# A two-layer hybrid decoder: conditioning products over all rows, more zero products, and other piece sizes in the first chunks

## The chip, the cores and the metric

The kernel runs on one core of one Trainium2 chip. The metric is the time of one execution on the device, in microseconds; the median of several runs is given. Five engines of the core work side by side: TensorE (PE in the profile; its weight loads are PEld), VectorE (DVE), ScalarE (ACT), GpSimd (POOL) and SyncE (SP), which here issues nearly all loads.

## The reference

A decoder trunk of two layers over one sequence of 256 tokens, width 1024, in float32. A layer is a SwiGLU block, a token mixer (layer 0: stick-breaking attention, layer 1: a gated linear recurrence, RG-LRU), and another SwiGLU block. Each block's input is normalised, scaled and shifted, and its output gated, by vectors that come from one conditioning vector c:

```python
c_act = jax.nn.silu(c)
for layer in range(DEPTH):
    mod = (c_act @ mod_w[layer] + mod_b[layer]).reshape(B, N_SUB, 3, D_MODEL)
    h, g = sublayer_input(x, norm_g[layer, 0], mod[:, 0])
    x = x + MACARON_W * g * swiglu(h, ffn_w_gu[layer, 0], ffn_w_down[layer, 0])
    ...
```

with `h = rmsnorm(x, g) * (1 + scale) + shift`, and `swiglu(h) = (silu(h @ w_g) * (h @ w_u)) @ w_down`. D_FF is 2816, the recurrent width 1280. The trunk ends with one RMSNorm.

## The kernel before

The activations lie transposed: eight tiles `x[d]` of 128 features by 256 tokens. Every weight is read once from memory, in blocks of 128 by 2048 (1 MB, the ring `raw` of three buffers, issued on SP). A float32 product is made of three products at the faster format: ScalarE rounds a piece of the block to `wh` (L536), VectorE takes the rest `wl = raw - wh` (L539), and the activations are split alike into a high and a low part (`hx`, made at L674 or L859). `group` (L565) issues wh by high, wh by low, wl by high. A *plain* group (L835) is instead one float32 product with the unsplit block and unsplit activations `h0`; it needs no split of the weights.

All operations are put on a list with costs and dependences, and `schedule` makes a plan from it: it walks in planned time, gives every operation a due time (`prio`, taken back from TensorE's order and its costs), and so fixes the order in which each engine's instructions are issued. `lat` overrides the planned time from one operation's end to its users' start. On the chip each engine works through its own list in that order and waits for semaphores; set-up instructions ahead of the list (memsets and casts on GpSimd and VectorE, L460 to L482) are not in the plan.

The start, in the first block of layer 0: ScalarE issues the load of c (one row, L1328) into a tile of the ring `rawm`; TensorE runs `EARLY` zero products (`warm`, L1323), and spreads c over 128 rows by a product with ones (L1337), in two halves of 512 columns. ScalarE takes SiLU of these into `cact` (`cond`). Meanwhile x comes in two halves; VectorE and ScalarE square it, VectorE folds the squares, TensorE sums them over the rows (L642), ScalarE makes the inverse root `rst` from that. A conditioning tile (`mod_tile`, L597) is a 128 by 1024 block of `mod_w`, 512 KB, multiplied by `cact` and summed by VectorE: eight results of a scale or shift vector. Two of them, w = 1 (scale) and w = 0 (shift), are needed for every chunk k of x. `hpre` is x[k] scaled (L668), from which ScalarE and VectorE make h.

The first block's products over the first eight column blocks (`SQ`) are ordered by chunk k of x, so that work can begin as soon as chunk 0 is there. Chunk k has 16 groups, in two halves of 1 MB loaded as pieces: chunks in `SMALL` in four pieces of 512 columns, the others in two of 1024. For chunk 0 the first `PLAIN` pieces go plain. Between the halves the load order puts the conditioning tiles of chunk k+1 (`early`). From the second set of column blocks on, all products run over whole column blocks.

At the end of the RG-LRU block, `output` (L1265) makes the operand of the last projection: for every pair n2 of blocks a product (L1275), a rounding on ScalarE, and the low part on VectorE (L1281).

Of the kernel before, what the change touches and what calls it, by code (L numbers as in the profile page):

```python
# [11 lines left out]
ALU = mybir.AluOpType  # L12
# [3 lines left out]
T = 256  # L16
TX = T + 2
D = 1024
# [5 lines left out]
NB = NR // 2  # L24
# [6 lines left out]
HALF = 1024  # L31
SQ = 8
NFIRST = 2
LAT0, RATE0, RATE = 950.0, 390.0, 360.0
SMALL = (0, 7)
EARLY, MID, LATE = 4, 3, 9
AHEAD = {(1, 0): 3}
KICK0, PLAIN = (1,), 2
HXPAD, HKPAD, ARPAD = 112, 16, 56
SKIP = 1  # L40

# [322 lines left out]
def c_dve(n):  # L364
    return 68.0 + 1.042 * n
# [11 lines left out]
def trunk(ctx, tc, xT, cb, par, modw, gu0, gu, wdn, qk, wv, wo, win, wri, wout, out):  # L377
    nc = tc.nc
    act, dve, pe, pool, sp = nc.scalar, nc.vector, nc.tensor, nc.gpsimd, nc.sync
    ctx.enter_context(tc.manual_schedule())  # L380
    pr = Program()
# [4 lines left out]
    def f32(ap):  # L386
        return ap.bitcast(F32)


    def ring(name, n, cols, dt=F32, pl=const, pitch=0):  # L390
        if pitch:
            whole = pl.tile([P, n * pitch], dt, tag=name, name=name)
            tiles = [whole[:, i * pitch : i * pitch + cols] for i in range(n)]
        else:
            tiles = [pl.tile([P, cols], dt, tag=f"{name}{i}", name=f"{name}{i}") for i in range(n)]
        return Space(name, n, lambda at, _: tiles[at]), tiles

    banks, _ = ring("bank", 8, 512, pl=psum)
    banks.exclusive = True
    rawr, _ = ring("raw", 3, CH)  # L400
    modr, _ = ring("rawm", 4, D)
    whr, _ = ring("wh", 7, HALF, F32R)
    wlr, _ = ring("wl", 7, HALF, F32R)
    const.tile([P, HXPAD], F32, tag="pad0", name="pad0")
    hxr, _ = ring("hx", 20, TX, F32R, pitch=320)
    const.tile([P, HKPAD], F32, tag="pad2", name="pad2")
    hkr, _ = ring("hk", 2, T, F32R)
    sqr, _ = ring("sq", 2, T)
    ssqr, _ = ring("ssq", 2, T)
    rmsr, _ = ring("rms", 1, T)  # L410
    rstr, _ = ring("rst", 1, T)
    hpr, _ = ring("hpre", 3, T)
    bcr, _ = ring("bc", 4, 2)
    tr, _ = ring("tr", 2, T)
    sgr, _ = ring("sg", 3, T)
# [6 lines left out]
    def new_phase(r_cells, f_cells, dts=(F32R, F32)):  # L422
        k = len(phases)
        prev = phases[-1]["spaces"] if phases else ()
        ph = {"size": (r_cells, f_cells), "dts": dts}

        def view(which):
            def v(at, n):
                enter(k)
                return phase["tiles"][which][:, at * CELL : (at + n) * CELL]  # L430
            return v

        ph["spaces"] = tuple(
            Space(f"ph{k}{n}", c, view(i), prev) for i, (n, c) in enumerate((("r", r_cells), ("f", f_cells))))
        phases.append(ph)
        return ph["spaces"]
# [15 lines left out]
    def fixed(name, cols, dt=F32):  # L452
        return const.tile([P, cols], dt, tag=name, name=name)
# [9 lines left out]
    ones = fixed("ones", P)  # L463
# [40 lines left out]
    def act_dma(dst, src, r, w, lat=2600.0):  # L504
        return pr.op("ACT", 60.0, lambda: act.dma_start(dst(), src), r, w, lat=lat)
# [6 lines left out]
    def V(fn, n, r, w, cost=None, ptr=0):  # L512
        return pr.op("DVE", cost or c_dve(n) + 62.0 * ptr, fn, r, w)
# [283 lines left out]
    def ffn(l, s, nxt, hook):  # L797
# [3 lines left out]
        else:  # L801
            R, _ = new_phase(2 * NF * 2 + AHEAD.get((l, s), 0) * 9, 0)
# [7 lines left out]
        if j == 0:  # L810
# [52 lines left out]
            for k in range(KD):  # L863
                if k == 0:
                    h0 = norm_chunk((0, 0), k, q, PLAIN > 0)
                    warm(LATE, [pr.last_pe])
                    for ks in xq_parts:
                        normed(ks)
                else:
                    first_chunk(k)  # L870
                size = HALF // 2 if k in SMALL else HALF
                done = [0]

                def chain(dst, src, n, w):
                    chained(dst, src, n, w, RATE0)
                    done[0] += n

                    if done[0] % HALF == 0:
                        for w in ((2 - done[0] // HALF,) if k < 3 else (1, 0) if done[0] == HALF else ()):
                            early(k + 1, w)  # L880

                plain = PLAIN if k == 0 else 0
                ws = load(gu0[k], CH, f"gu0_{k}", chain, size, plain)
                for f in range(SQ):
                    for g in range(2):
                        i, c0 = divmod((f * 2 + g) * P, size)
                        if i < plain:
                            plain_group(accs[f], g, *ws[i], (f * 2 + g) * P)
                            continue
                        group(accs[f], (g, 0), lambda b, g=g: b[:, g * T : (g + 1) * T], ws[i],  # L890
                              lambda u, c0=c0: u[:, c0 : c0 + P], hcur[0, 0][k], lambda v: v[:, :T], T, k == KD - 1)
                        if k in KICK0 and f == g == 0:
                            kick_op(accs[f], 0, (0, 0))
            chained(lambda: pars()[:, NP0:], par, NPAR - NP0, [(pars, 1)])
            R, _ = new_phase(2 * NF * 2, 0)
# [244 lines left out]
    def rglru(l, s, nxt):  # L1140
# [124 lines left out]
        def output(n2):  # L1265
            g, t = gt[n2], th[n2]
            tt = [(t, 0), (t, 1)]
            if n2 >= NB - KEEP:
                b, g = g, rr[n2]
                rg = [(g, 0), (g, 1)]  # L1270
                A(g, b, AF.Gelu_apprx_tanh, 2 * T, [(b, (0, 0)), (b, (1, 0))], rg, table="gelu", psum=True, after=sqs)
            else:
                rg = [g]
                A(g, g, AF.Gelu_apprx_tanh, 2 * T, [g], [g], table="gelu", after=sqs)
            V(lambda: dve.tensor_tensor(t(), t(), g(), ALU.mult), 2 * T, tt + rg, tt)  # L1275
            if n2 < N32:
                y = t
            else:
                y = Buf(R, 4), Buf(R, 4)
                A(y[0], t, AF.Copy, 2 * T, tt, [y[0]])  # L1280
                V(lambda: dve.tensor_tensor(y[1](), t(), f32(y[0]()), ALU.subtract), 2 * T, tt + [y[0]], [y[1]])  # L1281
            for e in range(2):
                ys.append((y, slice(e * T, (e + 1) * T)))

# [29 lines left out]
    def chained(dst, src, n, w, rate=RATE):  # L1314
        last[:] = [dma(dst, src, n, w, last, LAT0, rate)]
# [10 lines left out]
    def first_loads(F):  # L1326
        c, b = Buf(modr), [Buf(banks), Buf(banks)]
        act_dma(lambda: c()[:1, :], cb, [], [c], 300.0)  # L1328

        def cond(h, after=()):  # L1330
            cs = slice(h * 512, (h + 1) * 512)
            A(lambda: cact()[:, cs], b[h], AF.Silu, 512, [b[h]], [(cact, h)], table="silu", psum=True, after=after)

        warm(EARLY)
        for h in range(2):
            cs = slice(h * 512, (h + 1) * 512)
            pr.op("PE", 1870.0, lambda h=h, cs=cs: pe.matmul(b[h]()[:, :], ones[:1, :], c()[:1, cs], start=True, stop=True),  # L1337
                  [c], [b[h]])
        cond(0)
        warm(MID, [pr.last_pe])  # L1340


        pairs = []
        for h, (scalar_, vector_, extra) in enumerate(((0, 2, 0), (2, 0, NP0))):
            d = 4 * h
            a0, n = d * T, 4 * T + extra
            chained(lambda a0=a0, n=n: xall[:, a0 : a0 + n], xT[:, a0 : a0 + n], n, x[d : d + 4] + [(pars, 0)] * h, RATE0)
            sq = Buf(F, 8)
            v0 = vector_ * T
            V(lambda sq=sq, a0=a0, v0=v0: dve.tensor_tensor(  # L1350
                sq()[:, v0 : v0 + 2 * T], xall[:, a0 + v0 : a0 + v0 + 2 * T], xall[:, a0 + v0 : a0 + v0 + 2 * T], ALU.mult),
              2 * T, x[d + vector_ : d + vector_ + 2], [(sq, "V")])
            for i in (scalar_, scalar_ + 1):
                o = A(lambda sq=sq, i=i: sq()[:, i * T : (i + 1) * T], x[d + i], AF.Square, T, [x[d + i]], [(sq, i)])
            if h == 1:
                cond(1, [o])
            p = Buf(F, 4)
            V(lambda sq=sq, p=p: dve.tensor_tensor(p(), sq()[:, : 2 * T], sq()[:, 2 * T :], ALU.add), 2 * T,
              [(sq, "V"), (sq, scalar_), (sq, scalar_ + 1)], [p])
            if h == 0:  # L1360
                pairs += [(p, slice(0, T)), (p, slice(T, 2 * T))]
            else:
                one = Buf(F, 2)
                fold = V(lambda p=p: dve.tensor_tensor(one(), p()[:, :T], p()[:, T:], ALU.add), T, [p], [one])
                pairs.append((one, slice(0, T)))
        ssq[0, 0] = tuple(pairs)
        pr.op("DVE", 80.0, lambda: dve.scalar_tensor_tensor(gbias(), col(OFF_MB + KD, KD), 1.0, col(OFF_NG, KD), ALU.add,
                                                            ALU.mult), [(pars, 0)], [gbias], [fold])
# [95 lines left out]
```

## Time and profile before

| | before |
|---|---|
| runs | 955.54 us median of 3 (954.9 to 956.22) |
| the profiled execution's own time | 955.21 us |
| its span, first to last instruction | 953.5 us |
| TensorE busy | 943.3 us (99%) |
| VectorE, ScalarE busy | 794.7, 568.5 us |
| memory read | 248.92 MB, 262 GB/s over the span |

Times in the profile are microseconds from the start of the span. A row of a timeline gives start, length, engine, line, operation, the tile it writes and the tile it reads, and in brackets how long the engine had been idle before and what ended that. Successive products of TensorE overlap, so the rate is read from starts, not from lengths. A row of groups gives busy time and the mean length of one in ns.

### The profile page before, as it was taken

What the parts mean: (1) busy time and instruction counts of PE and PEld (TensorE: products, weight loads), DVE (VectorE), ACT (ScalarE), POOL (GpSimd) and SP (SyncE); (2) the same over time, 40 slices, a digit from 0 to 9 for tenths busy, and PEclk for the clock granted to TensorE, in tenths of its full rate; (3) what the DMA queues carried; (4) which work ended last, traced back from release to release, by engine and by line L of the source; (5) the groups of instructions that cost most, each with busy time, mean ns of one, the idle gap of its engine ahead of it and who ended that gap; (6) DMA issues with size and microseconds to landing.
All of it is one profiled execution on the core that took longest, in us unless ns stands there. A gap on an engine that the chain in (4) does not pass through costs nothing.

```text
span 953.5 us, 19706 instructions
## 1 busy us (share of the span) xinstructions
PE 943.3 (99%) x8124; PEld 932.3 (98%) x8124; DVE 794.7 (83%) x1291; ACT 568.5 (60%) x925; POOL 2.4 (0%) x15
## 2 busy tenths in 40 slices
PE   9999999999999999999999999999999999999996
PEld 6999999999999999999999999999999999999996
DVE  7999888899999998888899998875998997555443
ACT  6685453479786755554466544535789676544343
POOL 1000000000000000000000000000000000000000
PEclk9999999999999999999999999999999999999999
DMA  9989889947754698889966999997253646545421
GB/s 349 406 314 364 322 327 358 363 147 265 259 200 155 223 362 331 322 303 349 363 256 255 335 359 333 353 337 280 90 179 131 222 175 234 210 179 206 170 110 45
DMA packets 47900, 251.25 MB, mean 264 GB/s; under 512 B 5313, under 2 KB 5953, under 8 KB 28098
## 3 DMA queue, kind: packets, MB, share of 16 engines
q1 hardware_dynamic: 47376, 249.46, 69.7%
q8 instruction: 63, 1.03, 0.4%
q10 hardware_dynamic: 434, 0.53, 0.2%
q14 instruction: 27, 0.22, 0.1%
HBM read 248.92 MB, written 1.05 MB: 262 GB/s over the span
## 4 chain that ended last, share of the span: by engine, by line
PE 90%; DVE 4%; DMA 3%; ACT 2%; issue 0%; SPq 0%; DVEq 0%
PE bank L565 85%; PE bank L950 2%; DMA raw<-in_gu 2%; DVE wl L539 1%; PE bank L1080 1%; PE bank L1023 1%; DMA arenar<-in_modw 1%; ACT arenaf L509 1%; DVE arenaf L1262 1%; PE bank L1058 1%; PE bank L1191 0%; ACT wh L536 0%; DVE arenar L1281 0%; DVE arenaf L1259 0%; PE bank L642 0%
## 5 line engine op out<-in xcount | busy, mean ns | idle before, releaser
L565 PE MATMUL bank<-hx,wh 128*128 128x256 f32 (+1 forms) x3284 | 565.0, 277 | 0.6 <-DVE hx L859 0.5
L536 ACT ACTIVATE wh<-raw 128x1024 fp32r<-128x1024 f32 (+1 forms) x326 | 336.0, 1050 | 285.9 <-PE bank L565 205.1
L565 PEld LDWEIGHTS bank<-hx,wh 128*128 128x128 f32 x3284 | 496.7, 188 | 1.3 <-DVE hx L859 1.0
L539 DVE TENSOR_TENSOR wl<-raw,wh 128x1024 fp32r<-128x1024 f32 (+1 forms) x326 | 387.8, 1210 | 114.9 <-ACT wh L536 112.2
L565 PE MATMUL bank<-hx,wl 128*128 128x256 f32 (+1 forms) x1650 | 456.8, 277 | 0.2 <-DVE wl L539 0.2
L565 PEld LDWEIGHTS bank<-hx,wl 128*128 128x128 f32 x1650 | 310.3, 188 | 0.4 <-DVE wl L539 0.4
L565 PE MATMUL bank<-arenar,wh 128*128 128x256 f32 x1696 | 289.3, 276 | 0.1
L565 PEld LDWEIGHTS bank<-arenar,wh 128*128 128x128 f32 x1696 | 255.5, 188 | 0.3 <-DVE arenar L1281 0.3
L565 PE MATMUL bank<-arenar,wl 128*128 128x256 f32 x848 | 234.1, 276 | 0.0
L597 DVE SCALAR_TENSOR_TENSOR rawm<-rawm,cact 128x1024 f32<-128x1024 f32 x128 | 154.5, 1218 | 8.8 <-DMA rawm<-in_modw 8.3
L565 PEld LDWEIGHTS bank<-arenar,wl 128*128 128x128 f32 x848 | 159.2, 188 | 0.0
L509 ACT ACTIVATE arenar<-a 128x256 fp32r<-128x256 f32 x88 | 35.2, 404 | 8.4 <-DVE a L790 8.2
L509 ACT ACTIVATE sg<-bank 128x256 f32<-128x256 f32 x82 | 30.0, 369 | 13.9 <-PE bank L565 13.9
L795 DVE TENSOR_TENSOR arenar<-a,arenar 128x256 fp32r<-128x256 f32 x88 | 36.3, 417 | 1.0 <-ACT arenar L509 1.0
L790 DVE TENSOR_TENSOR a<-bank,sg 128x256 f32<-128x256 f32 x82 | 33.9, 416 | 0.2
L712 DVE SCALAR_TENSOR_TENSOR x<-bank,mf,x 128x256 f32<-128x256 f32 x48 | 21.5, 477 | 9.1 <-PE bank L565 9.1
L509 ACT ACTIVATE hx<-x,mf 128x256 fp32r<-128x256 f32 x40 | 18.5, 500 | 17.2 <-DVE x L712 17.2
L950 PE MATMUL bank<-wh,hx 128*128 128x256 f32 x128 | 24.2, 284 | 0.2 <-DVE arenar L1088 0.2
L509 ACT ACTIVATE hx<-hpre,mf 128x256 fp32r<-128x256 f32 x41 | 19.5, 498 | 5.8 <-DVE hpre L668 5.8
L509 ACT ACTIVATE arenaf<-bank 128x384 f32<-128x384 f32 (+1 forms) x37 | 17.7, 505 | 6.2 <-DVE arenaf L1262 2.8
L950 PEld LDWEIGHTS bank<-wh,hx 128*128 128x128 f32 x128 | 20.0, 188 | 0.7 <-DVE arenar L1088 0.5
L1407 ACT ACT_TABLE_LOAD x15 | 19.2, 1283 | 1.6 <-PEq L1452 1.3
(123 smaller groups left out, 541.1 us busy)
## 6 DMA issues: line engine op xcount, KB each, us to landing
raw<-in_gu SPq DMA_DIRECT2D x79, 1024.0 KB, 5.2
rawm<-in_modw SPq DMA_DIRECT2D x128, 512.0 KB, 6.5
raw<-in_wdn SPq DMA_DIRECT2D x44, 1024.0 KB, 4.9
raw<-in_win SPq DMA_DIRECT2D x10, 1024.0 KB, 5.0
arenar<-in_modw SPq DMA_DIRECT2D x16, 512.0 KB, 10.2
raw<-in_qk SPq DMA_DIRECT2D x8, 1024.0 KB, 4.8
raw<-in_gu SPq DMA_DIRECT2D x14, 512.0 KB, 10.2
raw<-in_wout SPq DMA_DIRECT2D x5, 1024.0 KB, 4.7
```

Of the source, the lines that this page charges most:

```text
L509: act.activation(o(), i(), f, **{k: (v() if callable(v) else v) for k, v in kw.items()})
L536: act.activation(h()[:, :m], raw()[:, a : a + m], AF.Copy)
L539: dve.tensor_tensor(lo()[:, :m], raw()[:, a : a + m], f32(h()[:, :m]), ALU.subtract)
L565: pe.matmul(o(b()), wc(u()), xc(v()), start=start and n == 0, stop=stop and n == len(passes) - 1, skip_group_check=True)
L597: dve.scalar_tensor_tensor(raw(), raw(), 1.0, cact(), ALU.mult, ALU.mult, accum_out=m()[:, t : t + 1])
L712: dve.scalar_tensor_tensor(x[d](), acc.b()[:, j * T : (j + 1) * T], gate()[:, d : d + 1], x[d](), ALU.mult, ALU.add)
L790: V(lambda: dve.tensor_tensor(a(), b()[:, T:], sg(), ALU.mult), T, [(b, (1, 0)), sg], [a])
L795: V(lambda: dve.tensor_tensor(y[1](), a(), f32(y[0]()), ALU.subtract), n, [a, y[0]], [y[1]])
L950: pe.matmul(o, u()[:, tb * P : (tb + 1) * P], v()[:, c0 : c0 + 256], start=start and n == 0, stop=k == KD - 1 and n == 2, skip_group_check ...
L1023: pe.matmul(zb[e]()[:, BL[i]], v()[rows, kc], w()[rows, qc], start=False, stop=i == 1 and n == 2, skip_group_check=True)
L1058: pe.matmul(b()[:, :S], ntri, hd(q(), e), start=False, stop=False, skip_group_check=True)
L1407: act.preload_act_table_set(TABLES[t])
```

## The change

1. `EARLY` goes from 4 to 8: eight zero products before the conditioning products.
2. The first tile of the ring `rawm` is set to zero by VectorE at the start; c still fills its first row. The product with ones then runs over all 128 rows of it instead of one.
3. `PLAIN` goes from 2 to 3: three of the four pieces of chunk 0 go plain.
4. `SMALL` takes in chunk 1: it is loaded and split in four pieces of 512 columns instead of two of 1024.
5. In the load order, chunks 3 and 4 get, like the earlier ones, one conditioning tile after each half instead of both after the first.
6. The last low part of the RG-LRU output (L1281, last n2) is planned with 900 ns instead of 170 ns to its users.

```diff
-SMALL = (0, 7)
-EARLY, MID, LATE = 4, 3, 9
+LASTY = 900.0
+SMALL = (0, 1, 7)
+EARLY, MID, LATE = 8, 3, 9
-KICK0, PLAIN = (1,), 2
+KICK0, PLAIN = (1,), 3
...
-    modr, _ = ring("rawm", 4, D)
+    modr, mods = ring("rawm", 4, D)
+    dve.memset(mods[0], 0.0)
...
-                        for w in ((2 - done[0] // HALF,) if k < 3 else (1, 0) if done[0] == HALF else ()):
+                        for w in ((2 - done[0] // HALF,) if k < 5 else (1, 0) if done[0] == HALF else ()):
...
-                V(lambda: dve.tensor_tensor(y[1](), t(), f32(y[0]()), ALU.subtract), 2 * T, tt + [y[0]], [y[1]])
+                pr.op("DVE", c_dve(2 * T), lambda: dve.tensor_tensor(y[1](), t(), f32(y[0]()), ALU.subtract), tt + [y[0]], [y[1]],
+                      lat=LASTY if n2 == NB - 1 else None)
...
-            pr.op("PE", 1870.0, lambda h=h, cs=cs: pe.matmul(b[h]()[:, :], ones[:1, :], c()[:1, cs], start=True, stop=True),
+            pr.op("PE", 1870.0, lambda h=h, cs=cs: pe.matmul(b[h]()[:, :], ones, c()[:, cs], start=True, stop=True),
                   [c], [b[h]])
```

## The prediction

> **What bounds the kernel now.** I read the page's busy times and chain first, then the list of waits of TensorE, the chain in order of time, and the timelines of the first 35 us.
>
> ```profile
> span 953.5 us, 19706 instructions
> ...
> PE 943.3 (99%) x8124; PEld 932.3 (98%) x8124; DVE 794.7 (83%) x1291; ACT 568.5 (60%) x925; POOL 2.4 (0%) x15
> ...
> PE 90%; DVE 4%; DMA 3%; ACT 2%; issue 0%; SPq 0%; DVEq 0%
> ```
>
> TensorE is the bound, and the time is its work plus what it loses before and between. Every edit but one acts in the first 45 us, so the question is where TensorE loses time there. The waits of TensorE, largest in the early part, and the chain in order of time:
>
> ```profile
> PE bank L835 <- ACT hpre L509: 0.6, 1, 0.6
> PE bank L565 <- DVE hx L859: 0.5, 1, 0.5
> PE bank L565 <- DVE wl L539: 0.2, 1, 0.2
> ```
>
> ```profile
> 16.29 11.25 DMA raw<-in_gu
> ...
> 30.31 2.28 DVE arenar L597 x3
> ...
> 32.69 1.15 DVE wl L539
> ...
> 33.88 166.54 PE bank L565 x1462
> ```
>
> From 33.88 us the chain is TensorE alone, 0.1139 us a product (166.54 / 1462), 0.342 us for the three products of a split group. So whatever the change does early is worth exactly what it moves TensorE's place at 33.88 us. TensorE's timeline up to there:
>
> ```profile
> 1.16 1.04 PE L1323 MATMUL bank<-zero 128*128 128x256 bf16 x4 [1.16 <-POOL eps L462]
> 2.30 3.75 PE L1337 MATMUL bank<-rawm,ones 1*128 1x512 f32 x4
> ...
> 6.60 2.85 PE L642 MATMUL bank<-arenaf,ones 128*128 128x256 f32 x6
> 9.24 2.13 PE L1323 MATMUL bank<-zero 128*128 128x256 bf16 x9
> 11.92 3.72 PE L835 MATMUL bank<-hpre,raw 128*128 128x256 f32 x16 [0.56 <-ACT hpre L509]
> ...
> 15.29 0.59 PE L565 MATMUL bank<-hx,wh 128*128 128x256 f32 x2
> ...
> 18.30 0.28 PE L565 MATMUL bank<-hx,wh 128*128 128x256 f32 x1
> 19.11 0.39 PE L565 MATMUL bank<-hx,wh 128*128 128x256 f32 x1 [0.53 <-DVE hx L859]
> ...
> 33.26 0.40 PE L565 MATMUL bank<-hx,wh 128*128 128x256 f32 x2
> ```
>
> Three places matter: the first plain product at 11.92 us; a hole before chunk 1 (from 18.30 to 19.11 us between two starts, where 0.114 is usual: 0.70 us lost); and a hole in chunk 3 (the second product of the pair at 33.26 starts near 33.38, the next at 33.88: 0.39 us lost).
>
> **What sets 11.92 us.** ScalarE and VectorE:
>
> ```profile
> 0.79 0.52 ACTq L505 DMA_DIRECT2D rawm<-in_cb  x1
> ...
> 1.34 1.28 ACT L1407 ACT_TABLE_LOAD   x1 [1.34 <-PEq L1452]
> ...
> 4.38 0.60 ACT L509 ACTIVATE cact<-bank 128x512 f32<-128x512 f32 x1 [1.76 <-PE bank L1337]
> ...
> 4.88 0.71 ACT L509 ACTIVATE arenaf<-x 128x256 f32<-128x256 f32 x2
> ...
> 5.62 0.69 DVE L1358 TENSOR_TENSOR arenaf<-arenaf 128x512 f32<-128x512 f32 x1 [0.49 <-ACT arenaf L509]
> ...
> 9.31 1.22 DVE L597 SCALAR_TENSOR_TENSOR arenar<-arenar,cact 128x1024 f32<-128x1024 f32 x1
> ...
> 10.78 0.48 DVE L668 SCALAR_TENSOR_TENSOR hpre<-x,mf,rst 128x256 f32<-128x256 f32 x1 [0.25 <-ACT mf L509]
> ...
> 11.36 0.51 ACT L509 ACTIVATE hpre<-hpre,mf 128x256 f32<-128x256 f32 x1 [0.43 <-DVE hpre L668]
> ```
>
> The conditioning products let ScalarE's first SiLU start at 4.38. The squares of x are queued behind it on ScalarE and end at 5.59 (4.88 + 0.71). VectorE waits for them (0.49 us), and from 5.62 works without a pause until 10.53 (9.31 + 1.22); hpre follows after 0.25, the plain product 1.14 later (11.92 - 10.78). So a conditioning vector that comes late moves the whole start one for one.
>
> **The clock.** The zero products at 9.24 lie (2.13 - 0.42) / 8 = 0.214 us apart, 0.42 being the length of one (four in 1.04 at the start: the same 0.21). A plain group is two records of two passes over 256 columns; the eight groups from 11.92 to 15.29 take 0.421 each, 0.105 a pass. So TensorE ran at half rate until about 11.4 us. The granted clock does not print it at the start, but prints the opposite change at the end (columns: stretch, length, busy PE, PEld, DVE, ACT, POOL with counts, granted clock, DMA share, GB/s):
>
> ```profile
> 4.60:8.00 3.40, 3.40 (x9) 1.50 (x7) 2.77 (x5) 3.10 (x7) 0.00 (x0) 1.00 1.00 391
> 8.00:11.40 3.40, 3.36 (x13) 1.86 (x11) 3.15 (x8) 1.77 (x6) 0.00 (x0) 1.00 0.88 286
> ...
> 947.10:950.50 3.40, 0.00 (x0) 0.00 (x0) 2.63 (x6) 0.23 (x1) 0.00 (x0) 1.00 0.46 170
> 950.50:953.50 3.00, 0.00 (x0) 0.00 (x0) 0.00 (x0) 0.00 (x0) 0.00 (x0) 0.50 0.45 157
> ```
>
> After 3.4 us of no product the clock is at 0.50. TensorE was busy all of 4.60 to 8.00, partly with products of one row, and the full rate did not come; after 8.00 to 11.40, busy with 128 rows, it came. I read this as: one-row products hardly count. The Trainium skill, "TensorE: Matmul & The Clock Gate", Part 1, says that a busy stretch of some 3.4 us releases the clock, and names busy time, not rows; this trace speaks against time alone. By the page's rule as it stands the wider products change nothing in the clock, which is the third rival below.
>
> **The change part by part.**
>
> *Zero products, memset, full rows.* Eight zero products end the earliest start of the conditioning products at 1.16 + 8 x 0.214 = 2.87 instead of 2.30. Rows cost nothing in time: 512 columns in two passes are four times 0.214 = 0.86, and the four one-row records lie (3.75 - 1.06) / 3 = 0.90 apart. The memset is a new first instruction of VectorE, idle then, so its own time is covered; but ScalarE's DMA of c writes the same tile and must wait for it. No memset of VectorE is in the trace; rows around it:
>
> ```profile
> L844 DVE TENSOR_TENSOR arenaf<-x,rst 128x1024 f32<-128x1024 f32 x1 | 1.2, 1217 | 0.0
> ...
> L480 DVE CAST mask<-a 128x256 bf16<-128x256 f32 x1 | 0.3, 294 | 0.4 <-POOL xb L482 0.4
> L475 DVE CAST ident<-a 128x128 bf16<-128x128 f32 x1 | 0.2, 207 | 0.0
> ```
>
> Casts grow by 87 ns per 128 columns, so 1024 take 0.82 us; a two-input operation takes 1.22. I take 1.2, the row of the same size. Starting at 0.8 like the other engines, c is issued at about 2.0 instead of 0.79, and the products start 1.5 later as before: 3.6 (the ends: 2.87, where TensorE's own zero products hold it, and 4.3, where the packet also queues behind x). Behind the waiting issue on ScalarE stands only the table load (1.28 us), which still ends near 3.9, before the SiLU. So everything from 4.38 on moves by 3.6 - 2.3 = 1.3 (0.6 to 2.0). In return the clock is released before the x statistics, whose products then take half the time, so that VectorE's work alone is late and the 0.25 before hpre goes. First plain product at 11.92 + 1.3 - 0.25 = 12.97: **+1.05** (+0.3 to +2.0).
>
> *Three plain pieces of four.* A piece holds four groups: 4 x 0.421 - 4 x 0.342 = **+0.32** on TensorE, all of it on its path. Off it come one split piece on ScalarE and VectorE. Raw buffer 0 is then read until about 16.4 by its first half, and chunk 3's load, issued at 16.29, may wait for that by a tenth or so; it lands 11.25 later behind a full queue, which covers it (nothing; 0.5 if the queue ran dry).
>
> *Chunk 1 in four pieces.* Two more issues on SP (0.33 us each, where SP mostly waits for landings), and two more splits per engine:
>
> ```profile
> L539 DVE TENSOR_TENSOR wl<-raw,wh 128x1024 fp32r<-128x1024 f32 x15 | 18.2, 1221 | 2.3 <-ACT wh L536 2.3
> L539 DVE TENSOR_TENSOR wl<-raw,wh 128x512 fp32r<-128x512 f32 x6 | 4.0, 686 | 0.1
> ```
>
> VectorE: 4 x 0.686 - 2 x 1.221 = +0.30, less 0.69 for the plain piece: -0.39. Nothing directly. The effect is at the first hole: chunk 0 took TensorE from 11.92 to 18.41 (one product after 18.30), so it now comes to chunk 1 at 12.97 + 6.49 + 0.32 = 19.78, 0.67 after the point (19.11) at which hx was ready before, and hx has less queued in front of it. The hole closes: **-0.70** (0 if hx slips with the start by as much).
>
> *One conditioning tile after each half, for chunks 3 and 4.* The second half of chunk 3 comes one tile earlier:
>
> ```profile
> 20.00:25.00 5.00, 5.00 (x46) 5.00 (x46) 4.70 (x8) 3.88 (x6) 0.00 (x0) 1.00 1.03 409
> ```
>
> 512 KB at 409 GB/s: 1.28 us. Its low part was ready at 33.84, so the hole in chunk 3 closes twice over, by the late TensorE and by this: **-0.39** (0 to -0.39). The other tile of chunk 4 comes 1.28 later; its two multiplies already stood back to back in VectorE's queue (30.31, 2.28 us), so nothing. What is late next is chunk 4's hx, with VectorE nearly full.
>
> *The last split of the RG-LRU.* Only the plan's latency changes; the operation may move ahead of others:
>
> ```profile
> PEld bank L565 <- DVE arenar L1281: 0.3, 1, 0.3
> ```
>
> ```profile
> 753.55 0.68 DVE L1281 TENSOR_TENSOR arenar<-arenaf,arenar 128x512 fp32r<-128x512 f32 x1
> ```
>
> At best the 0.3 goes, at worst the 0.68 of its own length is put before a weight split that TensorE then waits for; I take **-0.1**.
>
> *The order.* The four zero products add 436 ns to TensorE's planned times, from which both queues are sorted. No row prices this; either sign, up to one hole of 0.70 per flip. I take nothing.
>
> **Sum:** +1.05 + 0.32 - 0.70 - 0.39 - 0.10 = +0.18 us. Against the profiled execution's own 955.21 (1.7 outside the span, unchanged) that is 955.4; the median of the three runs shown is 955.54, so this is no change. 0.2% (1.9 us) is about what a measurement of this kernel can tell from none.
>
> **The rivals.**
>
> *The conditioning does not hold the start* (0.20). If ScalarE's squares come ahead of the SiLU, or c's packet is fast, VectorE starts as before and only the clock's gain is left: -0.25 + 0.32 - 0.70 - 0.39 - 0.25 = -1.27, 953.9. For it: VectorE was waiting 0.49 us for those squares. Against: on ScalarE the squares stand behind the SiLU, and the planned landing of c is not changed. Half of it falls beyond 0.2%, with a little from the order.
>
> *The clock falls back* (0.12): the slower side. At full rate the third statistics product and nine zero products are done near 11, and TensorE then idles 2 us of the last 3.4 before 12.97. An empty stretch brought 0.50 at the end; 3.36 of 3.40 brought full rate; 1.4 of 3.4 lies between. If it falls, the plain products run 3.4 us at half rate: +1.7, 957.1. It decides where fewer products than about a third of a stretch are enough to lose it. Half of it is beyond 0.2%.
>
> *Full rows don't release the clock earlier* (0.08), so that edit doesn't do what it says: the 0.25 stays, 955.6.
>
> *VectorE's queue opens holes in the chunks* (0.12). VectorE is 4.70 of 5 busy there, and each chunk's hx waits for two multiplies; three holes of 0.70 in chunks 2 to 7 give +2.1, 957.5. Against: it has 0.39 less to do, and TensorE comes later.
>
> **How the numbers follow.** The forecast, 955.4, has 0.48; its own range is 954.6 to 956.4 from the ends of the start (+0.3 to +2.0) and holes that stay in part. Faster by over 0.2%: half the first rival and 0.02 of the forecast, 0.12. Slower: 0.05 of the clock, 0.10 of the queue, 0.02 of a very late start, 0.17. Within: 0.71. The range that leaves out about a tenth on each side is 953.5 to 957.6.
>
> **What would show it.** Right: c's issue on ScalarE near 2.0, products from about 3.6, the SiLU near 5.7; statistics products at half their length; first plain product near 13.0 with twelve groups; no wait for hx at chunk 1 and none for wl in chunk 3; TensorE alone from there. Wrong: first plain product before 12.2 or after 13.9; plain groups at 0.84 us; new waits of TensorE after 34 us; a longer chain around the last split of the RG-LRU.

## The result: slower by 1.5 us

| | before | changed |
|---|---|---|
| median of 17 runs each | 955.71 us (954.9 to 961.61) | 957.21 us (956.89 to 958.39) |
| ratio | | 1.0015, 95% interval 1.0008 to 1.0022 |
| profiled execution: its own time, span | 955.21, 953.5 us | 957.01, 955.3 us |

The change costs 0.15%. That is inside the wide range given (953.5 to 957.6) and outside the forecast's own (954.6 to 956.4); the forecast was no change, and the interval excludes none. The page of the changed kernel, and its chain in order of time (start, length, what):

```profile
span 955.3 us, 19711 instructions
...
PE 97%; DVE 1%; ACT 1%; DMA 0%; issue 0%; DVEq 0%; ACTq 0%
```

```profile
1.08 0.91 DVE rawm L403
2.02 4.05 DMA rawm<-in_cb
6.21 2.06 PE bank L1340 x2
9.53 0.69 DVE arenaf L1361
...
15.49 5.45 PE bank L837 x24
20.94 1.73 PE bank L567 x15
22.71 179.67 PE bank L567 x1581
```

Before, the chain ran through loads and splits until 33.88 us. Now it opens with the memset and the load of c, reaches the first plain product at 15.49, and is TensorE from there. (All lines after the memset are two or three higher than before: L567 is the old L565.) The same in the timelines of VectorE, ScalarE and TensorE:

```profile
1.08 0.91 DVE L403 MEMSET rawm<- 128x1024 f32 x1 [1.08 <-PEq L1455]
...
2.02 0.53 ACTq L507 DMA_DIRECT2D rawm<-in_cb  x1
...
6.21 3.75 PE L1340 MATMUL bank<-rawm,ones 128*128 128x512 f32 x4 [3.16 <-DMA rawm<-in_cb]
...
8.29 0.60 ACT L511 ACTIVATE cact<-bank 128x512 f32<-128x512 f32 x1 [4.43 <-PE bank L1340]
...
9.53 0.69 DVE L1361 TENSOR_TENSOR arenaf<-arenaf 128x512 f32<-128x512 f32 x1 [4.40 <-ACT arenaf L511]
...
14.36 0.48 DVE L670 SCALAR_TENSOR_TENSOR hpre<-x,mf,rst 128x256 f32<-128x256 f32 x1
```

c is issued at 2.02, as forecast, but TensorE waits for it until 6.21, 4.19 us after the issue; before it was 2.30 - 0.79 = 1.51. The SiLU, the squares and VectorE's fold follow one for one (VectorE idle for 4.40 us), and the first plain product comes 3.57 us later than before: at 15.49, past the 13.9 that the prediction had named as a sign of being wrong.

As a marker of TensorE's place behind the early part I use the first product of the attention block's value projection, the first number after the durations:

```profile
L950 PE MATMUL bank<-wh,hx x128: 276/279/388, 206.4 to 281.9; 128*128 128x256 f32 x128
```

```profile
L952 PE MATMUL bank<-wh,hx x128: 276/279/392, 208.4 to 283.9; 128*128 128x256 f32 x128
```

The first is the kernel before, the second the changed one: +2.0 of the +3.57 is left there, and the spans end +1.8 apart. TensorE's waits in the changed kernel are only these in the early part, beside its first instruction's and one of 0.7 for the statistics; no hx or wl is among them:

```profile
PE bank L1340 <- DMA rawm<-in_cb: 3.2, 1, 3.2
PE bank L837 <- ACT hpre L511: 1.7, 1, 1.7
```

### The profile page after: what moved, and what is told of

It is laid out like the page before. It is cut to its first block, busy times and chain, and to the rows that moved or that the text cites. A ratio compares the mean times of both kernels' runs of the same rounds, so it can differ in the third digit from the quotient of the medians.

```text
span 955.3 us, 19711 instructions
## 1 busy us (share of the span) xinstructions
PE 941.2 (99%) x8124; PEld 931.5 (98%) x8124; DVE 795.0 (83%) x1293; ACT 567.3 (59%) x926; POOL 2.4 (0%) x15
## 4 chain that ended last, share of the span: by engine, by line
PE 97%; DVE 1%; ACT 1%; DMA 0%; issue 0%; DVEq 0%; ACTq 0%
PE bank L567 90%; PE bank L952 2%; PE bank L1193 1%; PE bank L1082 1%; PE bank L1025 1%; PE bank L837 1%; PE bank L1060 1%; DMA rawm<-in_cb 0%; PE bank L644 0%; PE bank L1062 0%; DVE arenar L599 0%; PE bank L1340 0%; DVE x L1305 0%; ACT arenar L511 0%; DVE arenaf L1361 0%
## 5 line engine op out<-in xcount | busy, mean ns | idle before, releaser
L567 PE MATMUL bank<-hx,wh 128*128 128x256 f32 (+1 forms) x3276 | 562.7, 277 | 0.0
L567 PEld LDWEIGHTS bank<-hx,wh 128*128 128x128 f32 x3276 | 495.0, 188 | 0.3
L567 PE MATMUL bank<-hx,wl 128*128 128x256 f32 (+1 forms) x1646 | 455.4, 277 | 0.0
L567 PEld LDWEIGHTS bank<-hx,wl 128*128 128x128 f32 x1646 | 309.5, 188 | 0.0
L567 PE MATMUL bank<-arenar,wh 128*128 128x256 f32 x1696 | 289.1, 276 | 0.0
L567 PEld LDWEIGHTS bank<-arenar,wh 128*128 128x128 f32 x1696 | 255.1, 188 | 0.0
L567 PE MATMUL bank<-arenar,wl 128*128 128x256 f32 x848 | 234.2, 276 | 0.0
L567 PEld LDWEIGHTS bank<-arenar,wl 128*128 128x128 f32 x848 | 159.2, 188 | 0.2 <-DVE wl L541 0.2
```

Of the source, the lines that this page charges most:

```text
L567: pe.matmul(o(b()), wc(u()), xc(v()), start=start and n == 0, stop=stop and n == len(passes) - 1, skip_group_check=True)
```

## The experiments

Three theories are told apart by these runs. Theory 1: c's load waits for the memset, then queues behind the loads of x and the first conditioning tiles; the start is late by that, and the chunk edits gain. Theory 2: the holes absorb the late start, and the chunk edits cost. Theory 3: the products over 128 rows cost.

**Chunk edits alone (chunks_only).**

```diff
-EARLY, MID, LATE = 8, 3, 9
+EARLY, MID, LATE = 4, 3, 9
-    dve.memset(mods[0], 0.0)
-            ... pe.matmul(b[h]()[:, :], ones, c()[:, cs], ...)
+            ... pe.matmul(b[h]()[:, :], ones[:1, :], c()[:1, cs], ...)
```

> The changed kernel without its first two edits: four zero products, no memset, one-row products; three plain pieces, chunk 1 in four pieces, the load order and the planned latency stay changed. Theory 1 (the start is late because c's load waits for the memset and then queues behind other loads; the chunk edits gain): first plain product at 11.9 us as before, no hole before chunk 1 nor in chunk 3, the first score-block product (206.4 before, 208.4 after) at 205.1 to 206.0, time 954.3 to 955.3. Theory 2 (the late start is absorbed by holes anyway and the chunk edits cost): first plain product at 11.9, first score-block product at 207.5 to 208.5, time near 957.

Measured: 955.63 against 955.55 us, ratio 0.9998 (0.9989 to 1.0006). First plain product at 11.93. Its marker and the waits in its timeline of TensorE:

```profile
L951 PE MATMUL bank<-wh,hx x128: 276/279/392, 206.7 to 282.1; 128*128 128x256 f32 x128
```

```profile
30.61 0.38 PE L566 MATMUL bank<-hx,wh 128*128 128x256 f32 x1 [0.32 <-DVE hx L860]
...
36.88 0.38 PE L566 MATMUL bank<-hx,wh 128*128 128x256 f32 x1 [0.36 <-DVE hx L860]
```

Neither theory's place (205.1 to 206.0; 207.5 to 208.5) came. The hole before chunk 1 is gone and the wait for wl in chunk 3 too, but chunks 3 and 4 now begin with waits for hx. The edits moved the holes; alone they gain nothing that can be told from none.

**Start edits alone (start_only).**

```diff
-EARLY, MID, LATE = 4, 3, 9
+EARLY, MID, LATE = 8, 3, 9
+    dve.memset(mods[0], 0.0)
-            ... ones[:1, :], c()[:1, cs] ...
+            ... ones, c()[:, cs] ...
```

> The kernel before with the first two edits alone: eight zero products, the memset, products over 128 rows. Theory 1: conditioning products at 6.2 us, first plain product near 15.5, both holes of the chunks closed by the late start itself, so that of 3.6 us about 1.5 to 2 remain: first score-block product at 207.9 to 208.5, time 957.0 to 957.7. Theory 2: first plain product near 15.5, but chunks that catch up: first score-block product within 0.4 of 206.4, time within 0.5 of the kernel before.

Measured: 958.14 us, ratio 1.0025 (1.0016 to 1.0034).

```profile
6.57 3.75 PE L1338 MATMUL bank<-rawm,ones 128*128 128x512 f32 x4 [3.52 <-DMA rawm<-in_cb]
```

```profile
L951 PE MATMUL bank<-wh,hx x128: 276/279/393, 209.6 to 285.1; 128*128 128x256 f32 x128
```

The start (15.85, 3.93 late) is as theory 1 has it, and both holes closed, but 3.2 us remain at the marker, more than the 1.5 to 2 expected. Theory 2 falls. Where the other microsecond went is seen in the rate of TensorE from 41 to 56 us, here and then before (busy PE with its count first):

```profile
41.00:56.00 15.00, 15.00 (x130) 15.00 (x129) 14.10 (x24) 11.09 (x20) 0.00 (x0) 1.00 0.76 286
```

```profile
41.00:56.00 15.00, 15.00 (x135) 15.00 (x134) 14.09 (x25) 11.57 (x23) 0.00 (x0) 1.00 0.87 327
```

No wait, no idle time, and yet 130 products instead of 135: the starts lie 0.1178 us apart instead of 0.1133, from a wait of 0.07 at 38.8 us to 66 us. That is about 1.0 us. With the 1.75 us of lateness that the holes take up, as found below, the marker comes out: 3.93 - 1.75 + 1.0 = 3.2. More on this slow rhythm below.

**The memset kept, one-row products (memset_one_row).** Only `ones, c()[:, cs]` goes back to `ones[:1, :], c()[:1, cs]`.

> The changed kernel with the memset kept but the product again over one row. Theory 1: the packet of c moves at 5.4 us as in the changed kernel, conditioning products at 6.2, first plain product at 15.5 to 15.9 (later if the clock is released later, since one-row products hardly count), time near 957.3. Theory 3 (the products over 128 rows are what costs): conditioning products at about 3, first plain product at 12 to 12.5, time 955 to 956.

```profile
6.34 3.75 PE L1340 MATMUL bank<-rawm,ones 1*128 1x512 f32 x4 [3.29 <-DMA rawm<-in_cb]
...
15.76 4.58 PE L837 MATMUL bank<-hpre,raw 128*128 128x256 f32 x20 [1.49 <-ACT hpre L511]
```

957.64 us in one run, marker at 208.7. The late start is there without the wide products, so theory 3 falls. That the load of c behind the memset is the cause is shown together with the next run, which takes that wait alone away.

**c loaded early, then copied (early_copy).**

```diff
     dve.memset(mods[0], 0.0)
+    act.dma_start(mods[1][:1, :], cb)
+    dve.tensor_copy(mods[0][:1, :], mods[1][:1, :])
-        act_dma(lambda: c()[:1, :], cb, [], [c], 300.0)
+        pr.op("ACT", 60.0, lambda: None, [], [c], lat=300.0)
```

> The changed kernel, with c loaded at once into another tile of the same ring and its row copied by VectorE into the zeroed tile, so that the load waits for nothing. Theory 1: conditioning products over 128 rows start at 3.0 to 3.8 us, first plain product at 12.3 to 13.2, first score-block product at 205.5 to 206.6, time 954.6 to 955.8. Theory 2 or 3 (chunk edits or full rows cost): conditioning products early too, but first score-block product at 207.5 or later, time near 957.

```profile
2.29 0.68 DVE L405 COPY rawm<-rawm 1x1024 f32<-1x1024 f32 x1 [0.30 <-DMA rawm<-in_cb]
...
3.12 2.64 PE L1342 MATMUL bank<-rawm,ones 128*128 128x512 f32 x4
5.60 0.49 PE L1328 MATMUL bank<-zero 128*128 128x256 bf16 x3
...
12.15 2.21 PE L839 MATMUL bank<-hpre,raw 128*128 128x256 f32 x9 [1.68 <-ACT hpre L513]
```

```profile
L954 PE MATMUL bank<-wh,hx x128: 276/279/393, 206.8 to 282.2; 128*128 128x256 f32 x128
```

955.4 against 955.55 us, ratio 1.0002 (0.9993 to 1.0011): without c's wait the whole loss is gone, all other edits kept. The copy waits for c until 2.29, 1.50 us after the issue at 0.79; in the kernel before, where the products do not wait for c, 1.51 was only the most that this load could have taken. The first plain product came a little before the expected 12.3, the marker 0.2 after its range, because the waits for hx of chunks_only are back (0.6 us in two).

**How long the wait is (short_wait, long_wait).** The kernel before with a memset ahead of c's load, of 256 columns, or twice the whole tile.

```diff
+    dve.memset(mods[0][:, :256], 0.0)     # short_wait
+    dve.memset(mods[0], 0.0)              # long_wait, twice
```

> The kernel before with a memset of 256 columns of c's tile in front of c's load, one-row products. The load is issued near 1.45 us instead of 0.79 (2.02 in the changed kernel). If the packet queues behind the loads of x and of the conditioning tiles issued before it: conditioning products at 3.5 to 5.0, between 2.3 and 6.3, more than 1.2 us later than before for 0.65 us of wait. If the load takes the same time whenever it is issued: conditioning products at 2.9 to 3.1.

> The kernel before with two whole memsets of c's tile in front of c's load, one-row products. The load is issued near 2.95 us. If the packet queues behind everything issued before it: conditioning products at 7.2 to 8.8, first plain product at 16.4 to 18. If there is one fixed delay in the busy stretch (3.4 us): conditioning products at 6.9 to 7.2.

Issue and conditioning products of short_wait, then of long_wait:

```profile
1.22 0.52 ACTq L506 DMA_DIRECT2D rawm<-in_cb  x1
...
4.77 3.75 PE L1338 MATMUL bank<-rawm,ones 1*128 1x512 f32 x4 [2.57 <-DMA rawm<-in_cb]
```

```profile
3.22 0.52 ACTq L507 DMA_DIRECT2D rawm<-in_cb  x1
...
7.45 3.75 PE L1339 MATMUL bank<-rawm,ones 1*128 1x512 f32 x4 [5.25 <-DMA rawm<-in_cb]
```

From issue to use: 1.50 us when issued at 0.79 (early_copy), 3.55 at 1.22, 4.23 at 3.22. Issued at 2.02 it was 4.19 in the changed kernel, 4.32 in memset_one_row, 4.55 in start_only, and 5.18 in start_kicks (further below):

```profile
7.20 3.75 PE L1338 MATMUL bank<-rawm,ones 128*128 128x512 f32 x4 [4.15 <-DMA rawm<-in_cb]
```

The packets in the traces say the same: c's 4 KB moved at 1.70 us in the kernel before, ahead of the first packets of the loads on SP at 1.80, but at 3.97 in short_wait, 5.42 in the changed kernel and 6.65 in long_wait. So this 4 KB load, issued into the running stream of other loads, took 2.0 to 3.7 us more, and 0.43 us of delay was enough for 2.0 of that; but it does not wait for all that was issued ahead of it, since the time levels off. The Trainium skill, "DMA: Bandwidth & Descriptors", Queues, rings and completion order, says that an engine takes turns between queues a packet at a time; a wait that levels off agrees with turns, not with one line for all. What one turn lasts, no run here shows.

The two runs also price lateness. The marker of short_wait, then long_wait:

```profile
L951 PE MATMUL bank<-wh,hx x128: 276/279/388, 207.1 to 282.6; 128*128 128x256 f32 x128
```

```profile
L952 PE MATMUL bank<-wh,hx x128: 276/280/388, 209.8 to 285.3; 128*128 128x256 f32 x128
```

Their first plain products came at 14.39 and 17.07, 2.47 and 5.15 late; at the marker 0.7 and 3.4 are left. So about 1.75 us of lateness is free, and the rest is paid in full. In neither run do TensorE's waits name hx or wl: the late start alone closes the holes. (955.93 and 958.62 us, one run each.)

**The load order (order_only, old_order).** The first is the kernel before with `k < 5`, the second chunks_only with `k < 3` put back.

> The kernel before with the new load order alone. If the order only moves the wait: no hole near 33.4, a hole of 0.3 to 0.6 us near 36.3 ahead of chunk 4 (wait for hx), the hole of 0.7 at 18.3 as before, first score-block product at 206.3 to 206.7. If the order gains as I forecast: no hole at 33.4 nor at 36.3, first score-block product at 205.9 to 206.1.

> The run with the chunk edits alone, and the load order put back too (both conditioning tiles after the first half for chunks 3 and 4). If the new load order makes the hole before chunk 4 (0.52 us at 36.25, TensorE waiting for hx), that hole goes, the hole for wl inside chunk 3 (0.38 at 33.4) comes back at least in part, and TensorE's place at the first score-block product is 206.2 to 206.7 (206.7 with the new order). If the finer pieces make it, the hole at 36.25 stays. Time 955.2 to 955.7.

Waits of TensorE in order_only, and the new one in its timeline; then the waits of old_order:

```profile
PE bank L565 <- DVE hx L859: 1.2, 3, 0.6
```

```profile
37.23 0.38 PE L565 MATMUL bank<-hx,wh 128*128 128x256 f32 x1 [0.48 <-DVE hx L859]
```

```profile
PE bank L566 <- DVE hx L860: 0.4, 2, 0.2
PE bank L566 <- DVE wl L540: 0.2, 1, 0.2
```

The order moves the wait, as expected: none for wl, and 0.48 us of idle for chunk 4's hx, whose shift tile is now loaded later. With the old order wl's wait is back and hx's smaller, but not gone. Both markers missed their ranges (208.1 and 207.9): both runs went at 130 products in 41 to 56 us, like start_only, which costs about 1 us. order_only is one run (957.27 us). old_order took 956.14 against 955.81 us, ratio 1.0006 (0.9993 to 1.002): unclear.

**The slow rhythm (start_kicks, kicks).** A 64-column product (a kick) after the first group of chunks 4 and 5, in start_only and in the kernel before.

```diff
-KICK0, PLAIN = (1,), 2
+KICK0, PLAIN = (1, 4, 5), 2
```

> The run with the start edits alone, with a short product of 64 columns (the kernel's own kick, used in chunk 1) also after the first group of chunks 4 and 5. In that run TensorE went at 0.1178 us a product from a small wait at 38.8 us to 66 us, where 0.1133 is usual. If a wait leaves TensorE in a slower rhythm that the short product breaks: 0.1133 from chunk 5 on, first score-block product at 208.5 to 208.8 instead of 209.6, times between 957.0 and 957.8. If the slow stretch comes from the data or the addresses of these chunks: 0.1178 up to 66 us, 209.6 to 209.8.

> The kernel before with the same two short products and nothing else. Each costs about 0.09 us. If the spread of the kernel before (954.9 to 957.4) comes in part from the slow rhythm after its holes, its higher times go and the median falls by 0.2 to 0.6 us (955.0 to 955.4); otherwise the median rises by 0.1 to 0.2.

The product group from 44 to 59 us (count, busy, mean ns), start_only, then start_kicks:

```profile
L566 PE MATMUL bank<-hx,wh 128*128 128x256 f32 x87 | 15.5, 281 | 0.0
```

```profile
L566 PE MATMUL bank<-hx,wh 128*128 128x256 f32 x89 | 15.4, 277 | 0.0
```

In start_kicks the starts are 0.1133 apart soon after its kick in chunk 4, at 39.8 us. But long_wait, which has no kick there, has a wait of 0.05 at its start of chunk 4, at 39.9, and is back at 0.1133 from 40.7 on:

```profile
41.00:56.00 15.00, 15.00 (x134) 15.00 (x134) 14.10 (x24) 11.70 (x21) 0.00 (x0) 1.00 0.68 255
```

It has the same weights and the same code for these chunks as start_only. So the slow rhythm does not come from these chunks as such, and that the kick ended it is not shown. The marker (209.5) missed, as its start was 0.6 later in this run. The times: 957.58 us, ratio 1.002 (1.0011 to 1.0029), an interval that overlaps the one of start_only. kicks gained nothing: 955.8 against 955.58, ratio 1.0008 (0.9995 to 1.0022). Its profiled run showed another thing:

```profile
7.38 0.72 ACT L509 ACTIVATE arenaf<-x 128x256 f32<-128x256 f32 x2 [1.70 <-DMA x<-in_xT]
...
10.39 2.12 PE L1323 MATMUL bank<-zero 128*128 128x256 bf16 x9
13.07 6.06 PE L835 MATMUL bank<-hpre,raw 128*128 128x256 f32 x16 [0.56 <-ACT hpre L509]
```

Sixteen plain records took 6.06 us instead of 3.72: with one-row products TensorE was at half rate until after 17 us in that execution (957.17 us), against 11.9 in the one shown of before. The plain products also began 1.15 us later, though nothing of the start was changed: ScalarE had to wait for the second half of x until 7.38 instead of 5.87. This execution prices lateness a third time: 1.15 + 2.34 - 1.75, and 0.14 for each of the two kicks (by the starts around them), are 2.0 us, and its marker is 1.9 late:

```profile
L950 PE MATMUL bank<-wh,hx x128: 276/279/388, 208.3 to 283.8; 128*128 128x256 f32 x128
```

**Everything together (early_kicks).** early_copy with `k < 3` and kicks in chunks 3 and 4.

> The run with c loaded early and copied (products over 128 rows from 3.1 us, clock released near 4.5), with the load order of the kernel before and a short product after the first group of chunks 3 and 4. If the spread of the kernel before comes from the clock's release (9 to 18 us after the start in one-row runs) and from the slow rhythm after holes, both are gone here: times within 0.6 us of each other, median 954.9 to 955.3, first score-block product at 206.3 to 206.9. If the clock and the rhythm do not make the spread, it stays as wide as before (954.9 to 957), median 955.4 to 955.9.

955.96 against 955.69 us, ratio 1.0 (0.9991 to 1.0009), times from 955.1 to 956.65, marker 207.0. It missed: times within 0.6 us of each other did not come, and no version can be told from the kernel before as faster.

## Why the prediction was wrong, step by step

- **c's wait: the step that failed.** The issue near 2.0 was right (the memset took 0.91, not 1.2, but began at 1.08, not 0.8). The flight after it was taken as 1.5 us, as before, with 4.3 as the latest start of the products. Issued at 2.02, with other loads streaming, it took 4.2 to 5.2 us (four kernels): products at 6.21 instead of 3.6. early_copy and memset_one_row show that this term alone turns the result.
- **From there to the plain product** the mechanism held: products +3.91, plain product +3.57; the 0.25 of the earlier clock was 0.34.
- **The plain piece:** 24 records from 15.49 to 20.59, 0.425 a group as taken (+0.32).
- **The holes** were named rightly but sized by their two largest gaps, 0.70 + 0.39. What a late start gets back is 1.75 us, by two runs and the profiled one of kicks: smaller waits around them and a slow rhythm (starts 0.118 us apart from 30.7 to 36.6 us) count too. With both sizes put right the sum reads 3.57 + 0.32 - 1.75 - 0.10 = +2.0, and the spans differ by 1.8.
- **Who closes them** was wrong: I gave it to the chunk edits as much as to the late start. Alone (chunks_only) they leave TensorE at +0.3, with new waits for hx, the one that I had named as late next. The first rival, 953.9 if c did not hold the start, falls with this: early_copy comes near that case (its first plain product is 0.23 late), and takes 955.4. (Its sum takes 0.25 off at the end without a reason; with the last split's 0.10 it would read 954.1.)
- **The clock** did come with wide products: the changed kernel's statistics took 1.13 us for four records, and the rival of the clock falling back did not happen: the plain groups are at full rate. But it did not come each time before the statistics: in start_kicks, with wide products from 7.20, most of them were still at half rate, and full rate came near 13.4. The Trainium skill's figure ("TensorE: Matmul & The Clock Gate", Part 1), some 3.4 us of busy time, agrees with early_copy, where full rate came between 4.1 and 4.7 us, TensorE having begun at 1.16; it does not agree with the one-row run at half rate beyond 17 us.
- **The last split** of the RG-LRU: TensorE's lateness goes from 2.0 to 1.9 us across it, the -0.1 taken.

## What to carry to other kernels

A wait added in front of a load can cost more than itself: the same 4 KB took 1.5 us ahead of the stream of loads and 3.6 to 5.2 us inside it. So what starts a chain is best issued first, into another tile than the one that must be zeroed, and is copied from there, as in early_copy. Where a chain of loads bounds the start and TensorE takes over later, lateness is free up to the sum of the holes (1.75 us here), and edits that close holes gain nothing beside it: each part has to be priced with the others as they will be, not added to them.

## What the runs showed of the hardware that was not expected

- TensorE's clock came later with one-row products. By the spacing of its products, full rate came 1.4 to 6.2 us after the first conditioning product in the five runs with 128-row ones, and 6.6 to 9.5 us after it in seven runs with one-row ones (over 15 in kicks). Counted from the first full-row product behind the one-row ones, these seven take 2.9 to 5.9 us: the one-row products seem hardly to count. The time also varies with the same start code: full rate near 9.0 us in old_order, 9.4 in chunks_only, 10.6 in order_only, 11.9 in the kernel before.
- TensorE can go on at 0.1178 us a product instead of 0.1133, for some 27 us, with no idle time in the profile. start_only, order_only and old_order did so after a wait at 36 to 39 us; the kernel before, chunks_only, short_wait and long_wait had waits at 36 to 40 us and did not. What sets it off and what ends it stay open.
- Part of the spread between runs lies in the start: the execution of kicks lost 1.15 us to x's second half and 2.34 to the clock, of which the holes took up 1.75. Whether that explains the other slow executions stays open; early_kicks, whose clock came near 6.1 us, still spread from 955.1 to 956.65.
- VectorE's memset of 1024 float32 columns took 0.91 us (four kernels), and of 256 columns 0.27 (short_wait).
